# Latent attention walked chunk by chunk of queries: VectorE sums the weights in PSUM, GpSimd makes the low parts, the value products run three tiles behind the scores

## The chip, the cores and the metric

The kernel is one program on one core of a Trainium2 chip. Its time is the device time of one execution in microseconds, the median of several runs. The core has TensorE (PE: matmuls, and PEld: their weight loads), VectorE (DVE), ScalarE (ACT), GpSimd (POOL) and SyncE (SP, which here issues DMAs). Each engine works through its own list of instructions in order, and waits at an instruction whose inputs or whose buffer are not ready.

## The reference, cut to what matters

One encoder layer over 1024 rows of one request and 256 of another. The part in question is the latent attention (MLA), 16 heads:

```
s = (einsum('bqhd,bkhd->bhqk', qn_b, k_nope) + einsum('bqhr,bkr->bhqk', qr_b, k_rope)) * scale
p = softmax(s, axis=-1)
o = einsum('bhqk,bkhd->bqhd', p, v)          # 16 heads, V_DIM 64, QK 64 + 32
```

The other parts (projections, dilated attention, gates, convolutional feed-forward, norms) are the same instructions in the same order on every engine before and after.

## The kernel before, in words

Products are made in three passes of float32r: an operand is split into a high part (a rounded copy) and a low part (the exact value minus the high part), and high x high, high x low and low x high are summed in PSUM.

The latent attention keeps the scores with keys on the partitions and queries along the row. A tile of scores is 128 keys x 512 queries. A head has 8 key tiles x 2 chunks of 512 queries for the long request, and one tile that holds both key blocks of the short one: 17 tiles a head, 272 in all. A tile takes these steps:

- three matmuls into a bank of tag `S` (`Head.scores`, L1171 to L1173); the third one also adds minus the row's maximum, from row 96 of `qL`
- `soft` (L1123): ACT makes `p` = exp (L1125) and `ph`, the same exp rounded to float32r (L1126); then the low part `pl` = `p` - `ph` (`sub_dve`, a helper on L78)
- the sum of the weights over the key tiles: POOL copies the first `p` of a chunk to `acc` (L1195) and adds the others (`pool_tt`, helper on L81); in the last two heads DVE adds every fourth
- the value products: two matmuls, `ph` and `pl`, into the `O` bank of that chunk (L1214, L1215); the weights of the matmul are `V`, high and low part side by side, so rows 0 to 63 and 64 to 127 of `O` are added at the end (`finish_o`: ACT L1135, then DVE)

Before, key tiles are the outer loop and the two chunks the inner one, so both chunks' `O` banks are open through a head; `pend` puts the value products of one key tile (two tiles of scores) behind the scores of the next.

`fill` puts other work between the tiles: the row maxima of the next head (`row_max`: one matmul into a bank of tag `mi`, L1106, and a `reduce_max` by DVE, L1107; at the end the two short ones, L1111 and L1112, a small maximum `nm`, and a transpose on PE, L1115, which ACT copies to `mr`), the projections of a later pair of heads (`project_pair`, into `mi` banks, L1076, which ACT and DVE split into `kH`/`kL` or `qH`/`qL`), and the sums of `acc` over partitions (`row_sums`, L1146). PSUM has eight banks: 3 `S`, 3 `mi`, 2 `O`. A scheduler orders each engine's instructions ahead of the run; the order on each engine is fixed in the program.

`value_load` (L1044) brings `V` for a pair of heads, one DMA of 10 KB a partition, two buffers.

Of the kernel before, what the change touches and what calls it, by code (L numbers as in the profile page):

```python
# [46 lines left out]
def kernel(  # L47
# [111 lines left out]
    def ada_chunk(c, load, banks_, tile_):  # L159
        """columns [512c, 512c+512) of the modulation, as per-partition columns of modT"""  # L160
        *ps, tp = banks_()
        tp = tp.rearrange("p (b n) -> p b n", b=4)
        for k in range(KD):
            j = k % 4
            w = load()
            nc.sync.dma_start(out=w, in_=ada_w[k * P:(k + 1) * P, 512 * c:512 * c + 512])
            nc.tensor.matmul(ps[k // 4][32 * j:32 * j + 32, :], lhsT=cT[:, k, :], rhs=w, start=True, stop=True,
                             tile_position=(0, 32 * j))
        rows = tile_()
        nc.scalar.copy(out=rows, in_=ps[0])  # L170
# [44 lines left out]
    # Winograd's form of Strassen's product: halves of the contraction, of a pair of blocks of features, of the tokens  # L215
# [6 lines left out]
    class Halves:  # L222
        """one split operand after another"""
# [30 lines left out]
    def product_set(raw, dst, mid, early=False):  # L254
        """dst = the product for two blocks of features"""
# [29 lines left out]
    # modulation, first norm, transposed activations  # L285
# [23 lines left out]
    def banks():  # L309
        """PSUM of a modulation chunk"""  # L310
# [73 lines left out]
    def values0(w):  # L384
        """values of the first group"""
# [37 lines left out]
    # projections: queries and keys of the dilated attention, latents; the values of the other groups meanwhile  # L423
# [19 lines left out]
    def sums(j):  # L443
        """the operands' sums, of one tile of each half of the contraction"""
# [56 lines left out]
    # dilated attention, gates  # L501
# [36 lines left out]
    def value_rows(g, b):  # L538
        """rows of a block of values"""
# [17 lines left out]
    def queries_keys(pair, g, res):  # L557
        """in the order of the classes, split"""
# [13 lines left out]
    def window(g, i):  # L572
        """first key of the window, query offset in it, value blocks as (index, column, keys)"""
# [21 lines left out]
    def block(w, to, m=P):  # L595
        """a block of features, multiplied plainly"""
# [24 lines left out]
    def rope(x, c, co, si, tiles):  # L621
        """rotation and split, in two steps"""
# [13 lines left out]
    def norms():  # L636
        """latents' norms, rotated part of the keys"""
# [84 lines left out]
    def gather(pair, full, gs):  # L722
        """least scores and sums of the groups, in the order of the tokens"""
# [16 lines left out]
    def combine(pair, full):  # L740
        """joint softmax weights of the three groups, merged output"""
# [174 lines left out]
    # the second branch's output projection, values of the latent attention, rotated parts of its queries  # L916
# [21 lines left out]
    def values_out(q, bank, stage, w):  # L938
        """split values of four heads, to DRAM"""
# [19 lines left out]
    def rope_q(j, w):  # L959
        """rotated parts of four heads' queries, to DRAM"""  # L960
# [62 lines left out]
    # latent attention  # L1023
# [6 lines left out]
    RATE = (3600, 700, 960, 960)  # L1030

    def mi():
        return mk(psM[1], [P, 512], tag="mi", bufs=3)
# [10 lines left out]
    def value_load(p_):  # L1044
        vts[p_] = mk(mpl, [P, NT, 2, 2, 64], F32R, tag="V", bufs=2)
        nc.sync.dma_start(out=f32(vts[p_]), in_=f32(v_d)[p_])
# [76 lines left out]
    def soft(ps):  # L1123
        p_, ph, pl = ms(tag="p", bufs=3), ms(F32R, "ph", 3), ms(F32R, "pl", 3)
        nc.scalar.activation(out=p_, in_=ps, func=AF.Exp, scale=MSCALE)  # L1125
        nc.scalar.activation(out=ph, in_=ps, func=AF.Exp, scale=MSCALE)  # L1126
        sub_dve(pl, p_, ph)
# [32 lines left out]
    class Head:  # L1160
        def __init__(self, h):
            self.h, self.hh = h, h % 2
            self.q, self.k, self.v = qts[h], kts[h], vts[h // 2]
# [11 lines left out]
        def w(self, kt):  # L1175
            return self.v[:, kt, self.hh].rearrange("p s d -> p (s d)")

        def step(self, kt, fill):
            """scores and weights of one key tile, or of the short group at the end"""
            got = []  # L1180
            if kt == NS:
                ps = mk(psM[1], [P, 512], tag="S", bufs=3)
                for j in range(2):
                    self.scores(ps[:, 256 * j:256 * j + 256], NS + j, SS, 256)
                e = soft(ps)
                pool_tt(self.acc[:, SS:T], e[0][:, 0:256], e[0][:, 256:512], ALU.add)
                fill()
                return [e]
            for c in range(2):
                ps = mk(psM[1], [P, 512], tag="S", bufs=3)  # L1190
                self.scores(ps, kt, 512 * c, 512)
                e = soft(ps)
                a = self.acc[:, 512 * c:512 * c + 512]
                if kt == 0:
                    nc.gpsimd.tensor_scalar(out=a, in0=e[0], scalar1=1.0, scalar2=1.0, op0=ALU.mult, op1=ALU.mult)  # L1195
                else:
                    (dve_tt if self.h >= NH - 2 and (2 * kt + c) % 4 == 3 else pool_tt)(a, a, e[0], ALU.add)
                got.append(e)
                fill()
            return got  # L1200

        def values(self, kt, es):
            if kt == NS:
                op = mk(psM[1], [P, 512], tag="O", bufs=2)
                for j in range(2):
                    for q in range(2):
                        nc.tensor.matmul(op[:, 0:256], lhsT=self.w(NS + j), rhs=es[0][1 + q][:, 256 * j:256 * j + 256],
# [3 lines left out]
            if kt == 0:  # L1211
                self.o = [mk(psM[1], [P, 512], tag="O", bufs=2) for _ in range(2)]
            for c in range(2):
                nc.tensor.matmul(self.o[c], lhsT=self.w(kt), rhs=es[c][1], start=(kt == 0), stop=False)  # L1214
                nc.tensor.matmul(self.o[c], lhsT=self.w(kt), rhs=es[c][2], start=False, stop=(kt == NS - 1))  # L1215
                if kt == NS - 1:
                    finish_o(self.o[c], self.h, 512 * c, 512)
# [6 lines left out]
    def stage(i):  # L1224
        return ms(F32R, ("ph", "pl", "p")[i % 3], 3)

    def ahead(jobs):
        """each job's weights are loaded before the job in front of it runs"""
# [24 lines left out]
    def prep(k, cs, stage, dst):  # L1253
        """normalised, split output of pair k for some chunks"""
# [96 lines left out]
    pend = None  # L1351
    for h in range(NH):
# [16 lines left out]
    pend[0].values(pend[1], pend[2])  # L1369
# [19 lines left out]
    # gated merge  # L1389
# [59 lines left out]
    def pa_early(m):  # L1449
        """weights in tiles that the later chunks' outputs take"""  # L1450
# [53 lines left out]
    # output projection, second norm  # L1504
# [38 lines left out]
    # the tokens are halved into (first half of the long request, of the short one) and the rest: HT columns each  # L1543
# [6 lines left out]
    def second(c, x2s):  # L1550
        """transposes of a chunk's rows, modulated; first halves are split"""
# [51 lines left out]
    # convolutional feed-forward, up: Winograd's form of Strassen's product, with the halves of the contraction,  # L1603
    # of a pair of blocks of features, and of the tokens
# [14 lines left out]
    def up_load(col):  # L1619
        """both halves of the contraction of two blocks of features, one of each half of them"""  # L1620
# [21 lines left out]
    # the first two blocks are multiplied plainly, while the operands' sums are made  # L1642
# [44 lines left out]
    def acts(p_, tt):  # L1687
        """the operands of the down product"""
# [52 lines left out]
    # down, in the same form, with the halves of the features, of the columns, and of the tokens; final norm  # L1741
# [97 lines left out]
    def gated(x, i, j, hs, ssq=None, early=False):  # L1839
        """half of the columns of x2 + gate * x"""  # L1840
# [132 lines left out]
```

## Time and profile before

| | |
|---|---|
| median of 3 runs | 2578.05 us (2569.92 to 2586.26) |
| the profiled execution, span of the program | 2573.2 us |
| latent attention, first scores to last value products | 895.8 to about 1461 us: 565 us |
| PE busy in that stage | 507.4 us of 565.2 |
| DVE busy in that stage | 531.8 us |
| POOL, ACT busy in that stage | 396.9 us, 354.7 us |

The profiled execution is given by its span; it lies 4.9 us below the median, inside the range of the runs. A matmul's end is modelled: one of 512 columns shows as 0.39 to 0.40 us, while the next one starts 0.23 us after it. So PE can be idle although its row of busy time is full, and waits of PE below about 0.16 us don't show. The head starts of the stage (first scores of each head) are at 895.83, 934.41, 969.67, 1000.20, 1040.35, 1070.97, 1109.58, 1140.14, 1180.33, 1211.02, 1249.61, 1280.20, 1316.07, 1346.76, 1382.33 and 1421.01 us.

### The profile page before, as it was taken

What the parts mean: (1) busy time and instruction counts of PE and PEld (TensorE: products, weight loads), DVE (VectorE), ACT (ScalarE), POOL (GpSimd) and SP (SyncE); (2) the same over time, 40 slices, a digit from 0 to 9 for tenths busy, and PEclk for the clock granted to TensorE, in tenths of its full rate; (3) what the DMA queues carried; (4) which work ended last, traced back from release to release, by engine and by line L of the source; (5) the groups of instructions that cost most, each with busy time, mean ns of one, the idle gap of its engine ahead of it and who ended that gap; (6) DMA issues with size and microseconds to landing.
All of it is one profiled execution on the core that took longest, in us unless ns stands there. A gap on an engine that the chain in (4) does not pass through costs nothing. (4 is left out here: it accounts for less than half of the span.)

```text
span 2573.2 us, 37087 instructions
## 1 busy us (share of the span) xinstructions
PE 2425.6 (94%) x13177; PEld 2009.6 (78%) x13177; DVE 1620.4 (63%) x2477; ACT 1085.4 (42%) x2106; POOL 1176.5 (46%) x826
## 2 busy tenths in 40 slices
PE   7899999999999989999998889998999999999997
PEld 4799996655578766666665678787999999988876
DVE  5733333343447799999999852548556556567668
ACT  4422123444434456666665543344223223244434
POOL 1543331100125177676777553026555654638473
PEclk9999999999999999999999899998999999999998
DMA  7233226566367923233332474351322322357554
GB/s 253 58 117 103 91 90 212 156 192 217 104 178 249 314 53 78 75 78 80 80 77 65 104 223 140 129 162 43 106 86 86 105 78 80 102 206 244 180 179 159
DMA packets 255187, 342.88 MB, mean 133 GB/s; under 512 B 24269, under 2 KB 157150, under 8 KB 253978
## 3 DMA queue, kind: packets, MB, share of 16 engines
q1 hardware_dynamic: 229358, 311.40, 39.2%
q10 hardware_dynamic: 25644, 29.12, 3.3%
q8 instruction: 103, 1.69, 0.3%
q14 instruction: 82, 0.67, 0.1%
HBM read 237.06 MB, written 94.19 MB: 129 GB/s over the span
## 5 line engine op out<-in xcount | busy, mean ns | idle before, releaser
L244 PE MATMUL X<-t,wh 128*128 128x320 f32 x2864 | 539.6, 310 | 8.0 <-ACT wh L230 4.1
L244 PEld LDWEIGHTS X<-t,wh 128*128 128x128 f32 x2864 | 452.2, 189 | 8.9 <-ACT wh L230 4.4
L81 POOL TENSOR_TENSOR acc<-acc,p 128x512 f32<-128x512 f32 x216 | 326.6, 1529 | 93.3 <-ACT p L1125 89.1
L244 PE MATMUL X<-t,wl 128*128 128x320 f32 x1432 | 328.2, 310 | 6.3 <-DVE wl L78 6.3
L78 DVE TENSOR_TENSOR pl<-p,ph 128x512 fp32r<-128x512 f32 x272 | 307.5, 1144 | 10.8 <-ACT ph L1126 8.8
L244 PEld LDWEIGHTS X<-t,wl 128*128 128x128 f32 x1432 | 240.2, 189 | 7.3 <-DVE wl L78 6.7
L1125 ACT ACTIVATE p<-S 128x512 f32<-128x512 f32 x272 | 163.6, 601 | 121.6 <-PE S L1173 63.5
L81 POOL TENSOR_TENSOR wl<-wr,wh 128x512 fp32r<-128x512 f32 (+2 forms) x50 | 68.1, 1363 | 301.8 <-ACT wh L209 272.0
L100 PE MATMUL pp<-t,wh 128*128 128x512 f32 (+3 forms) x672 | 199.8, 378 | 3.1 <-DVE sm L892 2.6
L78 DVE TENSOR_TENSOR ut<-X,ut 128x640 f32<-128x640 f32 x126 | 101.5, 820 | 138.3 <-PE X L244 85.8
L230 ACT CAST wh<-wr 128x512 fp32r<-128x512 f32 x113 | 70.1, 621 | 272.9 <-PE X L244 183.4
L1107 DVE TENSOR_REDUCE m<-mi 128x1 f32<-128x512 f32 x256 | 171.5, 681 | 17.7 <-PE mi L1106 16.7
L1126 ACT ACTIVATE ph<-S 128x512 fp32r<-128x512 f32 x272 | 162.9, 599 | 20.5 <-PE O L1214 20.2
L81 POOL TENSOR_TENSOR wl<-R,wh 128x512 fp32r<-128x512 f32 x63 | 103.3, 1640 | 145.4 <-ACT wh L230 145.4
L1798 PE MATMUL Y<-bh,ah 128*128 128x512 f32 x385 | 152.0, 395 | 7.7 <-DVE ut L78 6.6
L1798 PE MATMUL Y<-bl,ah 128*128 128x512 f32 x385 | 152.1, 395 | 6.3 <-POOL bl L81 6.3
L100 PEld LDWEIGHTS pp<-t,wh 128*128 128x128 f32 (+1 forms) x672 | 111.3, 185 | 56.4 <-issue 28.4
L1798 PE MATMUL Y<-bh,al 128*128 128x512 f32 x385 | 151.6, 394 | 0.0
L78 DVE TENSOR_TENSOR wl<-wr,wh 128x512 fp32r<-128x512 f32 x119 | 112.2, 943 | 53.5 <-ACT wh L230 48.9
L244 PE MATMUL X<-R,wh 128*128 128x320 f32 x736 | 139.3, 311 | 0.0
L78 DVE TENSOR_TENSOR pt<-X,pt 128x640 f32<-128x640 f32 x60 | 48.6, 823 | 135.2 <-PE X L244 83.8
L78 DVE TENSOR_TENSOR al<-ar,ah 128x640 fp32r<-128x640 f32 x75 | 89.2, 1191 | 59.7 <-ACT ah L1772 57.1
(438 smaller groups left out, 5773.3 us busy)
## 6 DMA issues: line engine op xcount, KB each, us to landing
ac_d<-ut SPq DMA_DIRECT2D x77, 320.0 KB
ar<-ac_d SPq DMA_DIRECT2D x75, 320.0 KB
R<-in_w_up_dram SPq DMA_DIRECT2D x84, 256.0 KB
br<-in_w_down_dram SPq DMA_DIRECT2D x77, 256.0 KB
ad<-in_ada_w_dram SPq DMA_DIRECT2D x64, 256.0 KB
wr<-in_w_in_dram SPq DMA_DIRECT2D x48, 256.0 KB
rw<-in_w_in_dram SPq DMA_DIRECT2D x20, 512.0 KB
V<-v_d SPq DMA_DIRECT2D x8, 1280.0 KB
```

Source lines behind the costliest of these rows:

```text
L78: nc.vector.tensor_tensor(out=out, in0=a, in1=b, op=op)
L81: nc.gpsimd.tensor_tensor(out=out, in0=a, in1=b, op=op)
L100: nc.tensor.matmul(ps, lhsT=w[k], rhs=x[k], start=(k == 0 and w is wh and x is xh), stop=(k == n - 1 and w is wl))
L230: nc.scalar.copy(out=h, in_=a)
L244: nc.tensor.matmul(ps[:, z, 0:320], lhsT=a[:, k, :], rhs=b[q][k][:, 320 * z:320 * z + 320], start=(j == 0 and i == 0), stop=(j == n - 1 an ...
L1107: nc.vector.reduce_max(out=m2[:, i, c:c + 1], in_=ps, axis=AX.X)
L1125: nc.scalar.activation(out=p_, in_=ps, func=AF.Exp, scale=MSCALE)
L1126: nc.scalar.activation(out=ph, in_=ps, func=AF.Exp, scale=MSCALE)
L1798: nc.tensor.matmul(ps, lhsT=a[:, P * j:P * j + P], rhs=b, start=(f == 0 and a is ah and b is bh), stop=(f == HF - 1 and a is al))
```

## The change

The chunk of queries becomes the outer loop: eight key tiles of chunk 0, eight of chunk 1, then the tile of the short request. One `O` bank is open at a time. The value products of a tile are issued after the scores of the third tile behind it (`LAG` 3).

The low parts `pl` of key tiles 1 to 7 go to POOL (224 of 272); those of key tile 0 and of the short tile stay on DVE. The sum of the weights goes to DVE: key tile 0 is only remembered, key tile 1 is added to it into a PSUM bank of the new tag `ac`, key tiles 2 to 6 are added in that bank in place, key tile 7 is added from the bank into `acc` in SBUF. That is 14 adds a head, 224 in all, of which 32 have both inputs in SBUF and 192 have the running sum in PSUM. POOL's 32 copies and 216 adds, and DVE's 8, go; the 16 adds of the short tile stay on POOL.

The bank for `ac` comes from `mi`, which has 2 banks now. `p`, `ph`, `pl` have 4, 5, 5 buffers (3 each before). `V` is loaded head by head, 16 DMAs of 640 KB in runs of 512 bytes, after the fifth tile of the head before.

```
+    PB, LAG = (4, 5, 5), 3
     def mi():
-        return mk(psM[1], [P, 512], tag="mi", bufs=3)
+        return mk(psM[1], [P, 512], tag="mi", bufs=2)
...
-    def value_load(p_):
-        vts[p_] = mk(mpl, [P, NT, 2, 2, 64], F32R, tag="V", bufs=2)
-        nc.sync.dma_start(out=f32(vts[p_]), in_=f32(v_d)[p_])
+    def value_load(h):
+        vts[h] = mk(mpl, [P, NT, 2, 64], F32R, tag="V", bufs=2)
+        nc.sync.dma_start(out=f32(vts[h]), in_=f32(v_d)[h // 2][:, :, h % 2])
...
-    def soft(ps):
-        p_, ph, pl = ms(tag="p", bufs=3), ms(F32R, "ph", 3), ms(F32R, "pl", 3)
+    def soft(ps, sub):
+        p_, ph, pl = ms(tag="p", bufs=PB[0]), ms(F32R, "ph", PB[1]), ms(F32R, "pl", PB[2])
         nc.scalar.activation(out=p_, in_=ps, func=AF.Exp, scale=MSCALE)
         nc.scalar.activation(out=ph, in_=ps, func=AF.Exp, scale=MSCALE)
-        sub_dve(pl, p_, ph)
+        sub(pl, p_, ph)
...
+        def step(self, c, kt):
+            ps = mk(psM[1], [P, 512], tag="S", bufs=3)
+            if c == 2:
                 for j in range(2):
                     self.scores(ps[:, 256 * j:256 * j + 256], NS + j, SS, 256)
-                e = soft(ps)
+                e = soft(ps, sub_dve)
                 pool_tt(self.acc[:, SS:T], e[0][:, 0:256], e[0][:, 256:512], ALU.add)
...
+            self.scores(ps, kt, 512 * c, 512)
+            e = soft(ps, sub_pool if kt else sub_dve)
+            if kt == 0:
+                self.first = e[0]
+            elif kt == 1:
+                self.sum = mk(psM[1], [P, 512], tag="ac", bufs=1)
+                dve_tt(self.sum, self.first, e[0], ALU.add)
+            else:
+                dve_tt(self.sum if kt < NS - 1 else self.acc[:, 512 * c:512 * c + 512], self.sum, e[0], ALU.add)
+            return e
...
+            nc.tensor.matmul(self.o, lhsT=self.w(kt), rhs=e[1], start=(kt == 0), stop=False)
+            nc.tensor.matmul(self.o, lhsT=self.w(kt), rhs=e[2], start=False, stop=(kt == NS - 1))
+            if kt == NS - 1:
+                finish_o(self.o, self.h, 512 * c, 512)
...
-    pend = None
+    pend = []
...
-        if h % 2 == 0 and h // 2 + 1 < KD:
-            value_load(h // 2 + 1)
         hd = Head(h)
-        for kt in range(NS + 1):
-            es = hd.step(kt, fill)
-            if pend is not None:
-                pend[0].values(pend[1], pend[2])
-            pend = (hd, kt, es)
+        for c, kt in [(c, kt) for c in range(2) for kt in range(NS)] + [(2, 0)]:
+            pend.append((hd, c, kt, hd.step(c, kt)))
+            fill()
+            if (c, kt) == (0, LAG + 1) and h + 1 < NH:
+                value_load(h + 1)
+            if len(pend) > LAG:
+                p_ = pend.pop(0)
+                p_[0].values(*p_[1:])
```

The lines of the helpers move by two or three: L1106 is L1107 after the change, L1214 is L1210, L1173 is L1174.

How the order moves, first on PE, in the middle of head 2 (heads are counted from 0). The row maximum and a projection stand between the scores `S` and the value products `O`; `waits` names the engine whose semaphore an instruction waits for. Before, two tiles' value products stand together, one behind the other chunk's:

```order
L1171 MATMUL S_1975_9560<-qH_1733_8757,kH_1716_8692 128x512 [waits Activation_49]
L1172 MATMUL S_1975_9560<-qH_1733_8757,kL_1717_8693 128x512
L1173 MATMUL S_1975_9560<-qL_1734_8758,kH_1716_8692 128x512
L1106 MATMUL mi_1979_9571<-kH_1731_8749,qH_1755_8843 128x512 [waits DVE_49]
L1076 MATMUL mi_1974_9556<-t_1413_7343,wh_1829_9079 128x256
L1076 MATMUL mi_1974_9556<-t_1416_7346,wh_1829_9079 128x256
L1076 MATMUL mi_1974_9556<-t_1413_7343,wl_1830_9080 128x256
L1214 MATMUL O_1957_9499<-ph_1961_9510,V_1703_8663 128x512
L1215 MATMUL O_1957_9499<-pl_1962_9511,V_1703_8663 128x512
L1214 MATMUL O_1958_9500<-ph_1966_9529,V_1703_8663 128x512 [waits Activation_49]
L1215 MATMUL O_1958_9500<-pl_1967_9530,V_1703_8663 128x512 [waits DVE_49]
```

Now, at the same place:

```order
L1172 MATMUL S_1980_9561<-qH_1733_8755,kH_1715_8689 128x512 [waits Activation_49]
L1173 MATMUL S_1980_9561<-qH_1733_8755,kL_1716_8690 128x512
L1174 MATMUL S_1980_9561<-qL_1734_8756,kH_1715_8689 128x512
L1107 MATMUL mi_1984_9572<-kH_1731_8747,qH_1755_8842 128x512 [waits DVE_49]
L1077 MATMUL mi_1979_9555<-t_1413_7343,wh_1830_9070 128x256
L1077 MATMUL mi_1979_9555<-t_1416_7346,wh_1830_9070 128x256
L1077 MATMUL mi_1979_9555<-t_1413_7343,wl_1831_9071 128x256
L1210 MATMUL O_1962_9499<-ph_1965_9507,V_1861_9166 128x512
L1211 MATMUL O_1962_9499<-pl_1966_9508,V_1861_9166 128x512 [waits Pool_49]
L1172 MATMUL S_1985_9580<-qH_1733_8755,kH_1715_8689 128x512 [waits Activation_49]
L1173 MATMUL S_1985_9580<-qH_1733_8755,kL_1716_8690 128x512
```

Every tile's scores are now followed by one tile's value products, those of three tiles earlier (`pl_1966` belongs to `S_1963`, the third `S` tile in front of `S_1980`), and the second of them waits for POOL where it waited for DVE. While the projection's `mi_1979` is open, one `mi` bank is left for the row maxima.

On DVE, in head 5, before: low parts `pl` (both inputs in SBUF) alternate with the reductions of the row maxima.

```order
L1107 TENSOR_REDUCE m2_2231_10419<-mi_2290_10600 128x1 [waits PE_49]
L78 TENSOR_TENSOR pl_2284_10576<-p_2282_10574,ph_2283_10575 128x512 [waits Activation_49]
L78 TENSOR_TENSOR pl_2289_10595<-p_2287_10593,ph_2288_10594 128x512 [waits PE_49,Activation_49]
L1107 TENSOR_REDUCE m2_2231_10419<-mi_2297_10620 128x1
L78 TENSOR_TENSOR pl_2296_10615<-p_2294_10613,ph_2295_10614 128x512 [waits DVE_49,PE_49,Activation_49]
L78 TENSOR_TENSOR pl_2302_10633<-p_2300_10631,ph_2301_10632 128x512 [waits PE_49,Activation_49]
L1107 TENSOR_REDUCE m2_2231_10419<-mi_2303_10638 128x1
```

Now the add of a tile's weights into `ac`, which waits for ACT's `p` of that tile, stands in front of the reduction of the row maximum that PE makes right behind the same tile's scores:

```order
L78 TENSOR_TENSOR ac_2289_10554<-ac_2289_10554,p_2300_10597 128x512 [waits DVE_49,Activation_49]
L1108 TENSOR_REDUCE m2_2244_10425<-mi_2303_10604 128x1 [waits PE_49]
L78 TENSOR_TENSOR ac_2289_10554<-ac_2289_10554,p_2306_10614 128x512 [waits DVE_49,Activation_49]
L1108 TENSOR_REDUCE m2_2244_10425<-mi_2309_10621 128x1 [waits PE_49]
L78 TENSOR_TENSOR ac_2289_10554<-ac_2289_10554,p_2313_10636 128x512 [waits DVE_49,Activation_49]
L1108 TENSOR_REDUCE m2_2244_10425<-mi_2316_10643 128x1 [waits PE_49]
```

Over the whole stage, 256 row maxima of 512 columns take an `mi` bank. After the change 93 of them take the bank that the row maximum just before used, and 107 that of the second before; with three banks one of them does the first, 75 the second and 121 the bank of the third before.

## Rows read from the trace of the kernel before

**Rows 1.** The page's first part: span, then busy time of each engine.

```profile
span 2573.2 us, 37087 instructions
PE 2425.6 (94%) x13177; PEld 2009.6 (78%) x13177; DVE 1620.4 (63%) x2477; ACT 1085.4 (42%) x2106; POOL 1176.5 (46%) x826
```

**Rows 2.** Busy time by stretch: stage, heads 4, 7, 14; columns named by its first line.

```profile
core 0: us, PE busy (x) PEld busy (x) DVE busy (x) ACT busy (x) POOL busy (x), PEclk, DMA share, GB/s
895.83:1461.00 565.17, 507.35 (x2158) 369.47 (x2156) 531.81 (x672) 354.70 (x692) 396.93 (x287) 0.96 0.29 74
...
1040.35:1070.97 30.62, 29.62 (x140) 21.94 (x138) 29.87 (x40) 21.43 (x43) 23.06 (x18) 1.00 0.55 139
...
1140.14:1180.33 40.19, 35.09 (x138) 25.71 (x137) 35.95 (x47) 22.41 (x45) 25.54 (x20) 0.92 0.07 19
...
1382.33:1421.01 38.68, 31.95 (x115) 19.92 (x113) 37.13 (x45) 22.60 (x44) 25.20 (x18) 0.87 0.24 73
```

**Rows 3.** Waits of PE and PEld in the stage: total us, times, longest.

```profile
PE O L1215 <- DVE pl L78: 15.5, 23, 1.9
PE mi L1115 <- DVE nm L1112: 14.2, 7, 3.0
PE mi L1106 <- DVE m L1107: 10.4, 14, 1.8
PE mi L1076 <- DVE kL L78: 3.1, 6, 0.6
PE O L1214 <- DVE ms L78: 2.3, 6, 0.4
...
PEld O L1215 <- DVE pl L78: 39.9, 60, 2.3
```

**Rows 4.** Groups by line and form, stage: count, busy us, mean ns, idle before.

```profile
L81 POOL TENSOR_TENSOR acc<-acc,p 128x512 f32<-128x512 f32 x216 | 326.6, 1529 | 93.3 <-ACT p L1125 89.1 <-PE mi L1076 1.9 <-DVE acc L78 1.3
L78 DVE TENSOR_TENSOR pl<-p,ph 128x512 fp32r<-128x512 f32 x272 | 307.5, 1144 | 10.8 <-ACT ph L1126 8.8
...
L1107 DVE TENSOR_REDUCE m<-mi 128x1 f32<-128x512 f32 x234 | 157.0, 681 | 17.6 <-PE mi L1106 16.7
...
L1195 POOL TENSOR_SCALAR acc<-p 128x512 f32<-128x512 f32 x32 | 23.3, 728 | 53.7 <-ACT p L1125 53.7
...
L78 DVE TENSOR_TENSOR acc<-acc,p 128x512 f32<-128x512 f32 x8 | 9.8, 1223 | 0.0
L78 DVE TENSOR_TENSOR nm<-m 128x8 f32<-128x8 f32 x15 | 9.6, 639 | 0.2
L78 DVE TENSOR_TENSOR kL<-mi,kH 128x512 fp32r<-128x512 f32 x14 | 9.6, 684 | 0.2
```

**Rows 5.** Timeline, head 7: start us, us, engine, line, names, count, idle before.

```profile
1156.44 0.50 PE L1106 MATMUL mi<-kH,qH 96*128 96x512 f32 x1 [1.17 <-DVE m L1107]
...
1156.91 1.80 DVE L78 TENSOR_TENSOR pl<-p,ph 128x512 fp32r<-128x512 f32 x1
...
1157.93 0.40 PE L1172 MATMUL S<-qH,kL 96*128 96x512 f32 x1
...
1158.17 0.40 PE L1173 MATMUL S<-qL,kH 97*128 97x512 f32 x1
...
1158.65 0.60 ACT L1125 ACTIVATE p<-S 128x512 f32<-128x512 f32 x1 [0.78 <-PE S L1173]
...
1159.24 0.67 DVE L78 TENSOR_TENSOR pl<-p,ph 128x512 fp32r<-128x512 f32 x1
...
1161.52 1.34 POOL L81 TENSOR_TENSOR acc<-acc,p 128x512 f32<-128x512 f32 x1 [0.47 <-PE mi L1076]
1161.63 0.68 DVE L1107 TENSOR_REDUCE m<-mi 128x1 f32<-128x512 f32 x1
```

**Rows 6.** Timeline, end of head 7's row maxima.

```profile
1164.27 1.83 DVE L78 TENSOR_TENSOR pl<-p,ph 128x512 fp32r<-128x512 f32 x1
...
1166.02 1.22 DVE L78 TENSOR_TENSOR nm<-m 128x8 f32<-128x8 f32 x1
...
1167.96 0.38 PE L1115 MATMUL mi<-t,nm 128*10 128x128 f32 x1 [2.11 <-DVE nm L1112]
```

**Rows 7.** Busy time in the stretch right behind, columns as in Rows 2.

```profile
1167.96:1174.79 6.83, 6.83 (x17) 5.36 (x18) 4.08 (x5) 2.55 (x5) 2.55 (x2) 0.51 0.01 2
```

More of the change, by code (lines that the diff above doesn't have):

```diff
@@ L1162, in __init__ @@
             self.h, self.hh = h, h % 2
-            self.q, self.k, self.v = qts[h], kts[h], vts[h // 2]
+            self.q, self.k, self.v = qts[h], kts[h], vts[h]
             self.acc = accs[h] = mk(mpl, [P, T], tag="acc", bufs=3)
@@ L1175, in w, with values @@
         def w(self, kt):
[L1176 to L1182, printed above, removed]
+            return self.v[:, kt].rearrange("p s d -> p (s d)")
+        def step(self, c, kt):
+            ps = mk(psM[1], [P, 512], tag="S", bufs=3)
+            if c == 2:
                 for j in range(2):
                     self.scores(ps[:, 256 * j:256 * j + 256], NS + j, SS, 256)
-                e = soft(ps)
+                e = soft(ps, sub_dve)
                 pool_tt(self.acc[:, SS:T], e[0][:, 0:256], e[0][:, 256:512], ALU.add)
[L1187 to L1203, printed above, removed]
+                return e
[8 more added lines that the diff above has]
+                dve_tt(self.sum if kt < NS - 1 else self.acc[:, 512 * c:512 * c + 512], self.sum, e[0], ALU.add)
+            return e
+        def values(self, c, kt, e):
+            if c == 2:
                 op = mk(psM[1], [P, 512], tag="O", bufs=2)
@@ L1206, in values @@
                     for q in range(2):
-                        nc.tensor.matmul(op[:, 0:256], lhsT=self.w(NS + j), rhs=es[0][1 + q][:, 256 * j:256 * j + 256],
+                        nc.tensor.matmul(op[:, 0:256], lhsT=self.w(NS + j), rhs=e[1 + q][:, 256 * j:256 * j + 256],
                                          start=(j == 0 and q == 0), stop=(j == 1 and q == 1))
@@ L1211, in values @@
             if kt == 0:
[L1212 to L1217, printed above, removed]
+                self.o = mk(psM[1], [P, 512], tag="O", bufs=2)
+            nc.tensor.matmul(self.o, lhsT=self.w(kt), rhs=e[1], start=(kt == 0), stop=False)
+            nc.tensor.matmul(self.o, lhsT=self.w(kt), rhs=e[2], start=False, stop=(kt == NS - 1))
+            if kt == NS - 1:
+                finish_o(self.o, self.h, 512 * c, 512)
     ready = set()
@@ L1224, in stage @@
     def stage(i):
-        return ms(F32R, ("ph", "pl", "p")[i % 3], 3)
+        return ms(F32R, ("ph", "pl", "p")[i % 3], PB[(1, 2, 0)[i % 3]])
     def ahead(jobs):
@@ L1358 @@
         side = [others(h), 0.0, 0.0, (h > 0) + max(0, h - NH + 3)]
-        if h % 2 == 0 and h // 2 + 1 < KD:
-            value_load(h // 2 + 1)
         hd = Head(h)
-        for kt in range(NS + 1):
-            es = hd.step(kt, fill)
-            if pend is not None:
-                pend[0].values(pend[1], pend[2])
-            pend = (hd, kt, es)
+        for c, kt in [(c, kt) for c in range(2) for kt in range(NS)] + [(2, 0)]:
[6 more added lines that the diff above has]
+                p_[0].values(*p_[1:])
         if h % 2 == 0 or h == NH - 1:
             run(side[0])
-    pend[0].values(pend[1], pend[2])
+    for p_ in pend:
+        p_[0].values(*p_[1:])
     zc = mk(mpl, [P, 2 * NT], tag="zc", bufs=2)
```

## The prediction, made before the changed kernel ran

> **What bounds the kernel now.** The page's first part [rows 1] shows PE busy for 94% of the span, which would make any saving on DVE worthless. But that is a mean over stages. The next view to read is busy time by stretch [rows 2]: in the latent attention DVE is busy 531.8 of 565.2 us, 94%, and PE 507.4. Head 7 takes 40.2 us, head 4 only 30.6: in both DVE is nearly full, and in head 7 PE is busy 35.1 of 40.2 at a mean granted clock of 0.92.
>
> How far PE is from its own limit needs the timeline, since busy rows of PE overlap: a matmul of 512 columns follows the one before after 0.23 us (second and third pass of a score tile) [rows 5]. By the program the stage has 768 of them for scores (3 for each of 256 tiles), 512 for values, 234 for row maxima [rows 4] and 210 for projections (7 pairs of heads, 15 matmuls for each of 2 chunks): 1724 x 0.23 = 397 us. Those of 256 columns are 96 + 64 + 30 + 105 = 295, at half of that 34 us; row sums and transposes I put at 25: about 455 us. So 110 of the 565 us are not work of PE. The granted clock explains a part: a mean of 0.96 [rows 2] is 4% lost, 23 us. The rest is waiting, and the list of waits [rows 3] says for whom: every large row of PE ends in DVE. DVE sets the pace of this stage, and PE is next.
>
> Why DVE is full is seen in two groups [rows 4]: 272 low parts at 1144 ns and 234 reductions at 681. Both have 512 elements a partition. The timeline shows the difference [rows 5]: a low part takes 0.67 us in one place and 1.80 in another, while a reduction that reads PSUM takes 0.68 with a POOL add running beside it. The low part reads two SBUF tiles; where POOL works on SBUF too, one waits for the other. POOL shows the other side: its add is 1.34 us beside the reduction [rows 5], 1529 ns in the mean [rows 4]. Head 7's end shows it at its worst [rows 6]: a low part of 1.83, then a maximum over 8 elements that takes 1.22, and PE stands 2.11 us at the transpose behind them; right after, the clock is granted at 0.51 for 6.8 us [rows 7].
>
> **The change, part by part.** The sum is made for the profiled execution, 2573.2 us, in this stage alone; outside it no order changes.
>
> *DVE's work.* 224 low parts go, 224 x 1.144 = 256, and 8 adds, 10. Of the 224 new adds, 32 read two SBUF tiles: 1.144 each, 37. The other 192 read the sum in PSUM. No row of before writes PSUM from DVE. The nearest is `kL<-mi,kH`, one input in PSUM and one in SBUF, at 684 ns; the dear end is the 1223 ns of the in-place add `acc<-acc,p` on DVE [rows 4]. I take 0.684, because the costly part is the second SBUF read and that is what goes: 131. DVE falls from 532 to 532 - 266 + 168 = 434 (537 at the dear end, the same as now).
> The Trainium skill (Perfetto Trace Analysis, Optimizing Scalar/DVE Operations) gives DVE a fixed overhead of some 60 ns an instruction on SBUF and 125 on PSUM. That is 65 ns more for each of the 192, 12 us as an estimate, and if all of it came onto the path the sum below would be -29 instead of -41; the rows here, 0.684 with PSUM against 0.67 for a low part alone, show no such difference.
>
> *POOL's work.* It loses 326.6 + 23.3 us [rows 4] and gets 224 low parts, two SBUF inputs each like its adds: 1.34 beside reductions, 1.53 in the mean of before. DVE's partners that read two SBUF tiles fall from 17 or more a head to 5 and the small maximum, so I take 1.34: 300. POOL goes from 397 to 347 (389 at the dear end): not the bound. ACT keeps its 355. The longest is then PE with 455.
>
> *What PE gets back.*
> 1. Waits of the value products for `pl` [rows 3]: 15.5 us by PE's rows. As a matmul's row is 0.16 us longer than its pitch, each of the 23 hides 0.16, 4 more; the weight loads show 37 further waits of which at most 0.16 each, 6, can be lost. 25 in all, between 15.5 and the 39.9 of the loads. All of it goes: from the third score pass to `p` are 0.48 us, two exponentials 1.2 [rows 5], the low part 1.34 to 1.8; ready after 3.0 to 3.5 us, wanted after three tiles, over 5. **-25**.
> 2. The transpose of the maxima: 14.2 us in 7 waits. Of head 7's 2.11 the low part's excess in front of `nm` goes, but `nm` reads two SBUF tiles and still meets POOL. **-9**, between 0 and -14.
> 3. The clock: the half clock stands behind these waits [rows 6, 7]. With half of the wait, about half of the 23: **-12**, between 0 and -23.
> 4. Late `kL`, `ms` and smaller ones, 5.4 in the rows shown, 3 more hidden under the pitch: **-5**, between 0 and -8.
> 5. Two `mi` banks instead of three. PE waits 10.4 us for `mi` now, 14 times. After the change 93 maxima follow the last one's reduction in the same bank. That reduction stands on DVE behind the tile's add, which waits for `p`: 1.08 us after the third score pass `p` is done, +0.68 add, +0.68 reduction, 2.45. PE's next maximum comes 6 matmuls (1.4 us) later without a projection between, 9 (2.1 us) with one. So up to 1.05 is short, but one wait delays the next tile's scores too and so pays for the next; and where PE's order puts the maximum behind the value products, nothing is short. 0.1 us each: **+9**; between 0 and, at the 1.17 us of the row [rows 5], +109.
> 6. At the end of the stage three tiles' value products stand behind the last scores instead of two: **+1**. `V` is issued 12 tiles, some 20 us, ahead of its use and moves half as much a time, in shorter runs; SP issues it when the value products of the head before last are done, which they are by then, so nothing queues behind it: 0.
>
> Sum: -25 - 9 - 12 - 5 + 9 + 1 = **-41**: a span of 2532. The span of before stands 4.9 us below the median of the runs, so **2537 us**. The stage would take 524 us, PE's 455 with 13% lost.
>
> **Rivals.**
> *The two `mi` banks bind (slower).* Without term 5 the change gives back 50. With 93 tight maxima it is lost when each costs 0.54 us more; at the 1.17 of the row [rows 5] it is 109 - 50 = +59, 2637 us. For it: the chain through the add is longer than a tile's matmuls, projections hold the other bank through most heads. Against: the waits overlap, and before, with 98% of DVE used in head 4, PE still was busy 29.6 of 30.6. I give 0.11 to slower, 0.12 to a cost near break-even (0.3 to 0.8 us each: 2556 to 2602).
> The Trainium skill (Perfetto Trace Analysis, Matmuls) wants independent groups of matmuls to rotate through different PSUM banks, so that evacuating one overlaps the next; taking a bank from `mi` goes against it, and the 1.17 us wait agrees.
>
> *DVE and POOL only swap.* If the add into PSUM meets POOL as the low part did, the 192 cost 1.144, DVE keeps 522 of its 532 us, and only 10 us come back: 2568. For it: no row shows DVE writing PSUM. Against: reading PSUM keeps 0.68 beside POOL. 0.10.
> The Trainium skill (the same page, Optimizing Scalar/DVE Operations) says that moving work between these two might not help, since they share an SBUF read port; the 1.80 and 0.67 us agree that they do, but its rule does not look at where the operands lie.
>
> *PE becomes the bound and runs through.* All of `pl` by the loads' rows 40, `nm` 14, clock 23, late ones 8, `mi` no dearer: -85, 2493. The stage would be at 480, PE at 95%. Head 4 of before comes near: 29.6 of 30.6 busy. 0.12 for under 2513.
>
> **The numbers.** My forecast, 2513 to 2552, has 0.55. A measurement here tells about 1% from no change, 26 us: faster is below 2552, slower above 2604. Faster: 0.55 + 0.12 = 0.67. Same: 0.12 + 0.10 = 0.22. Slower 0.11. The range reaches from 2500, which leaves out 0.06 of the best case, to 2590, which leaves out the slower rival: 0.12.
>
> **What would show it.** Adds named `ac` at 0.68 us on DVE, not 1.1; low parts on POOL at 1.3 to 1.4; no wait of the value products for POOL worth naming; DVE busy about 434 in the stage, 83% of it; odd heads down from 39 to some 34 us, even ones unchanged or a little longer; the transpose's wait near 1 us and fewer stretches at half clock. The forecast is wrong if the row maxima's wait for DVE exceeds 30 us in PE's rows, if `ac` adds cost over 1 us, or if POOL is busy over nine tenths and the value products wait for it.

## The result and the profile after

The changed kernel takes 2507.3 us (median of 4 runs, 2504.9 to 2509.3), the kernel before in the same comparison 2574.4 (4 runs, 2569.9 to 2586.3). The ratio is 0.9732, 95% interval 0.9711 to 0.9753: 67 us less, where 41 were forecast and 2500 to 2590 us was the range. It lies below the 2513 to 2552 us that the prediction calls its forecast, in the part under 2513 that it gave 0.12. A second comparison gave 2507.8 us, ratio 0.9738 (0.9716 to 0.9760).

The page's first part answers to [rows 1]:

```profile
span 2505.9 us, 37001 instructions
PE 2396.6 (96%) x13177; PEld 2006.3 (80%) x13177; DVE 1508.6 (60%) x2469; ACT 1081.3 (43%) x2106; POOL 1114.5 (44%) x802
```

Its PE row says as little as that of before: 94% became 96% with the same 13177 matmuls. The stage shows the change. Busy time by stretch, columns as in [rows 2]: the stage, then heads 4, 7 and 14.

```profile
906.60:1393.40 486.80, 470.57 (x2148) 361.07 (x2146) 416.37 (x661) 349.97 (x692) 335.04 (x263) 0.99 0.34 89
1027.96:1057.35 29.39, 29.34 (x140) 22.27 (x139) 24.70 (x41) 21.49 (x44) 18.55 (x15) 1.00 0.52 127
1117.80:1148.26 30.46, 30.09 (x137) 23.75 (x136) 27.22 (x45) 21.81 (x44) 21.50 (x17) 1.00 0.14 40
1321.80:1357.40 35.60, 28.89 (x119) 19.57 (x118) 32.36 (x46) 23.62 (x49) 27.84 (x22) 0.95 0.36 107
```

The stage fell from 565.2 to 486.8 us, 78 less, and DVE in it from 531.8 to 416.4. Head 7 is down from 40.2 to 30.5 us, head 4 from 30.6 to 29.4; its PE is now busy 29.34 of 29.39. Head 14 is now the dearest. The clock of the stage went from 0.96 to 0.99. That the time fell by 67 and not 78 lies ahead of the stage: it begins at 906.6 us instead of 895.8, at a mean granted clock up to there of 0.97 instead of 0.98. In the eleven traces of the experiments below it begins between 900.3 and 906.6, at 903.6 in the one of the kernel before with one number changed. So I take this for scatter and not for a doing of the change. The 78 of the stage, from one trace of each kernel, is uncertain by a few us: a second trace of the changed kernel has 490.5 us. Behind the last value products the span is the same to 0.5 us: 1113.5 and 1113.1 (the two stretches end 1.3 and 0.6 us behind them).

Waits of PE and PEld in the stage, to be laid beside [rows 3] (total us, times, longest):

```profile
PE O L1211 <- POOL pl L81: 4.0, 6, 1.0
PE mi L1116 <- DVE nm L78: 3.3, 7, 0.8
PE O L1210 <- issue: 2.5, 1, 2.5
...
PE mi L1112 <- DVE m L1108: 1.3, 1, 1.3
PE mi L1077 <- DVE m L1108: 1.0, 2, 0.8
...
PEld mi L1107 <- DVE m L1108: 12.4, 42, 0.8
PEld O L1211 <- POOL pl L81: 9.5, 14, 1.5
```

The value products waited 15.5 us for a low part, now 4.0 (loads: 39.9, now 9.5). The transposes waited 14.2, now 3.3. The row maxima waited 10.4 us for a bank, with three banks; with two, no row of PE for them is left among the large ones.

Groups by line and form, to be laid beside [rows 4] (count, busy us, mean ns, idle before):

```profile
L81 POOL TENSOR_TENSOR pl<-p,ph 128x512 fp32r<-128x512 f32 x224 | 298.0, 1339 | 135.8 <-ACT ph L1127 110.3 <-PE mi L1107 4.8 <-PE S L1173 4.6
...
L1108 DVE TENSOR_REDUCE m<-mi 128x1 f32<-128x512 f32 x234 | 159.3, 686 | 32.4 <-PE mi L1107 29.8
L78 DVE TENSOR_TENSOR ac<-ac,p 128x512 f32<-128x512 f32 x160 | 111.0, 694 | 9.1 <-ACT p L1126 7.1
L78 DVE TENSOR_TENSOR pl<-p,ph 128x512 fp32r<-128x512 f32 x48 | 40.1, 836 | 9.3 <-ACT ph L1127 6.9 <-ACT qH L1083 0.7 <-POOL pl L81 0.6
L78 DVE TENSOR_TENSOR ac<-p,p 128x512 f32<-128x512 f32 x32 | 24.9, 780 | 0.8 <-ACT p L1126 0.8
L78 DVE TENSOR_TENSOR acc<-ac,p 128x512 f32<-128x512 f32 x32 | 22.0, 686 | 2.6 <-ACT p L1126 1.6
```

The three kinds of add point to the mechanism: with the running sum in PSUM 686 to 694 ns, with both inputs in SBUF 780. And POOL idles 136 us in front of its low parts, most of it until ACT has made the next `ph`: it is early, not late.

The end of head 7's row maxima, where [rows 6] had 1.83, 1.22 and 2.11 us, on DVE and then on PE (start us, us):

```profile
1140.28 0.73 DVE L78 TENSOR_TENSOR nm<-m 128x8 f32<-128x8 f32 x1
1140.93 0.69 DVE L78 TENSOR_TENSOR ac<-ac,p 128x512 f32<-128x512 f32 x1
```

```profile
1141.06 0.28 PE L1116 MATMUL mi<-t,nm 128*10 128x128 f32 x1 [0.37 <-DVE nm L78]
```

The maximum over 8 elements still meets POOL (0.73 us; 0.17 in the mean where POOL is nearly idle, in the experiment with all low parts on DVE), but nothing long stands in front of it. The transpose waits 0.37 us instead of 2.11, and the half clock that followed [rows 7] is gone.

### The profile page after: what moved, and what is told of

Read it like the earlier page. It is cut to its first block, busy times and chain, and to the rows that moved or that the text cites. A ratio compares the mean times of both kernels' runs of the same rounds, so it can differ in the third digit from the quotient of the medians.

```text
span 2505.9 us, 37001 instructions
## 1 busy us (share of the span) xinstructions
PE 2396.6 (96%) x13177; PEld 2006.3 (80%) x13177; DVE 1508.6 (60%) x2469; ACT 1081.3 (43%) x2106; POOL 1114.5 (44%) x802
## 5 line engine op out<-in xcount | busy, mean ns | idle before, releaser
L81 POOL TENSOR_TENSOR pl<-p,ph 128x512 fp32r<-128x512 f32 x224 | 298.0, 1339 | 135.8 <-ACT ph L1127 110.3
L81 POOL TENSOR_TENSOR wl<-wr,wh 128x512 fp32r<-128x512 f32 (+2 forms) x50 | 62.9, 1258 | 310.7 <-ACT wh L209 281.2
L100 PE MATMUL pp<-t,wl 128*128 128x512 f32 (+3 forms) x336 | 123.2, 367 | 0.0
```

The costliest lines, as they stand in the source:

```text
L81: nc.gpsimd.tensor_tensor(out=out, in0=a, in1=b, op=op)
L100: nc.tensor.matmul(ps, lhsT=w[k], rhs=x[k], start=(k == 0 and w is wh and x is xh), stop=(k == n - 1 and w is wl))
```

## The experiments

The theory (A): before, DVE is full, because its low parts read two SBUF tiles beside a POOL that does the same; the sum in PSUM and the low parts on POOL take it out of the limit, and three tiles of distance cover POOL's slower low part. The rivals: the order and the distance alone do it (B); it does not matter where the sum lies (C); and, from the prediction, the two `mi` banks cost. Ratios are to the kernel before; its median was 2575.5 us.

**The value products one tile behind.**

```
-    PB, LAG = (4, 5, 5), 3
+    PB, LAG = (4, 5, 5), 1
```

> The changed kernel with the value products one tile behind the scores (LAG 1) in place of three. Theory A (VectorE's pace was set by instructions that read two SBUF tiles beside GpSimd; the sum in PSUM frees it, TensorE becomes the bound): a low part is ready some 3.1 us after the third score pass (0.48 to p, 1.2 for two exponentials, 1.34 on GpSimd); with one tile of lag two tiles then take at least 3.1 + 0.23 + 0.7 = 4.0 us, 2.0 a tile for the 1.79 of now, so +40 to +65 us on 2507: 2545 to 2575. Theory B (the lag is what gave the gain, the swap of work is even): all of the gain goes, 2575 or more, and the waits of the value products for the low parts account for all of it.

Measured: 2568.7 us, ratio 0.9979 (0.9970 to 0.9988). The stage's busy times (columns as in [rows 2], here and in all such rows below):

```profile
902.99:1454.88 551.89, 505.91 (x2148) 355.41 (x2146) 415.89 (x661) 353.83 (x691) 335.29 (x263) 0.99 0.31 78
```

Its waits for the low part:

```profile
PE O L1211 <- POOL pl L81: 37.3, 72, 1.3
...
PEld O L1211 <- POOL pl L81: 93.5, 151, 1.7
```

The time is in A's range. DVE is as free as in the changed kernel (415.9 us), and all but 7 us of the gain are lost: the new split of the engines is worth little without the distance. A low part on POOL takes 1.33 us instead of DVE's 0.7, and PE's loads now wait for it 151 times. (The load of `V` hangs on `LAG` too; it moves from behind the fifth tile to behind the third.)

**The new order with the old engines.** Low parts on DVE, sum on POOL in SBUF, three `mi` banks; chunk order, distance of three and buffers of the change.

```
-            e = soft(ps, sub_pool if kt else sub_dve)
+            e = soft(ps, sub_dve)
+            a = self.acc[:, 512 * c:512 * c + 512]
...
-                dve_tt(self.sum if kt < NS - 1 else ..., self.sum, e[0], ALU.add)
+                (dve_tt if self.h >= NH - 2 and (8 * c + kt) % 4 == 3 else pool_tt)(a, a, e[0], ALU.add)
```

> The changed order (chunk by chunk, lag 3, V by head, the buffers of the change) with the work of VectorE and GpSimd as before: all low parts on VectorE, the sum on GpSimd in SBUF, three mi banks (the ac bank isn't needed). Theory A: VectorE is busy about 530 us in the stage again and the stage is near 540 to 560 us; only the waits for low parts (about 25 us) can go: 2545 to 2572. Theory B: the order and the lag carry the gain: 2505 to 2525.

Measured: 2557.6 us, ratio 0.9942 (0.9921 to 0.9962), in A's range. The stage, and PE's largest wait:

```profile
902.05:1442.37 540.32, 493.55 (x2143) 370.93 (x2141) 503.45 (x667) 350.84 (x691) 395.69 (x287) 0.95 0.31 80
```

```profile
PE O L1209 <- DVE pl L78: 14.8, 15, 5.5
```

Theory B falls: order and distance alone bring 18 us of the 67. DVE is busy 503.5 of 540.3 us, the low part takes 1046 ns in the mean, and PE still waits 14.8 us for it.

**The running sum in SBUF**, the same adds on the same engine:

```
-                self.sum = mk(psM[1], [P, 512], tag="ac", bufs=1)
+                self.sum = self.acc[:, 512 * c:512 * c + 512]
```

> The changed kernel with one thing undone: VectorE keeps the running sum in SBUF (acc) and not in PSUM, so all 224 adds read two SBUF tiles. Same counts on every engine, mi still 2 banks. Theory A: adds take 1.1 to 1.3 us for 0.69, low parts on GpSimd 1.5 to 1.65 for 1.34, VectorE is busy about 510 us: 2540 to 2570. Rival C (the gain is that the work is spread evenly; where the sum lies does not matter): 2505 to 2515, adds at 0.7.

Measured: 2564.7 us, ratio 0.9963 (0.9950 to 0.9975). C falls. In the stage (547.8 us) DVE is busy 499.1. The two groups that meet:

```profile
L81 POOL TENSOR_TENSOR pl<-p,ph 128x512 fp32r<-128x512 f32 x224 | 336.3, 1513 | 151.5 <-ACT ph L1127 125.4 <-PE O L1211 11.4 <-PE S L1173 8.8
L78 DVE TENSOR_TENSOR acc<-acc,p 128x512 f32<-128x512 f32 x192 | 219.2, 1142 | 7.1 <-ACT p L1126 4.5
```

And the largest waits, of PE and of its loads:

```profile
PE mi L1107 <- DVE m L1108: 20.1, 43, 1.7
...
PEld mi L1107 <- DVE m L1108: 55.8, 94, 2.2
```

The same add costs 1142 ns instead of 690, the low part on POOL 1513 instead of 1339, and DVE is full again. Putting this one tile back costs 57 us. Taking away the distance cost 61 and the engines' split 50: each part needs the others, so these figures do not divide the 67 among them. The Trainium skill (SBUF — State Buffer, Who interferes with whom) says that a DVE instruction with at most one SBUF input, outside the modes that use two ports, does not contend with GpSimd; the 694 ns beside these 1142 agree with it.

**Two `mi` banks in the kernel before.**

```
-        return mk(psM[1], [P, 512], tag="mi", bufs=3)
+        return mk(psM[1], [P, 512], tag="mi", bufs=2)
```

> The kernel before with two mi banks in place of three and nothing else. My prediction put +9 us on this in the changed kernel. If the cost of a bank depends on how late VectorE is, it is larger here, where VectorE is 94% busy: 2585 to 2615 (before 2574), with TensorE's waits for the row maxima well over 10 us. If two banks do whatever VectorE does, 2570 to 2580.

Measured: 2579.6 us, ratio 1.0015 (1.0003 to 1.0028). The stage, and the waits for `mi`:

```profile
903.65:1467.20 563.55, 512.33 (x2156) 354.91 (x2155) 527.82 (x670) 352.88 (x692) 392.42 (x287) 0.98 0.29 75
```

```profile
PE mi L1106 <- DVE m L1107: 14.5, 42, 1.2
...
PE mi L1115 <- DVE nm L78: 2.6, 3, 1.3
...
PE mi L1115 <- DVE nm L1112: 0.9, 4, 0.2
...
PEld mi L1106 <- DVE m L1107: 53.8, 105, 1.6
```

Two rows of the kernel before, beside those of [rows 3]:

```profile
PE mi L1115 <- DVE nm L78: 1.6, 3, 0.9
...
PEld mi L1106 <- DVE m L1107: 19.8, 24, 2.1
```

The waits of the row maxima grow (from 10.4 in PE's rows, from 19.8 in the loads'), but the stage stays at 563.5 us, and the time is in the range put for "two banks do whatever VectorE does". What PE loses at the maxima it gains at the transposes, which wait 3.5 us instead of 15.8: with DVE full, what PE waits for in one place it need not wait for in another. The expectation of a loss that grows with DVE's lateness was too high.

**All low parts on DVE**, the sum in PSUM:

```
-            e = soft(ps, sub_pool if kt else sub_dve)
+            e = soft(ps, sub_dve)
```

> The changed kernel with all 272 low parts of the stage on VectorE; the sum stays in PSUM, so GpSimd keeps only 16 small adds of the stage and the preparation of the next one. Theory A (low parts are long because GpSimd works on SBUF beside them; VectorE, when full, sets the pace): low parts fall to 0.67 to 0.72 us, and VectorE has 272 x 0.68 = 185, sums 155, reductions 159 and 59 of other work of the changed kernel, 558 us, more than the 532 of before: it is full again, stage 560 to 590, 2575 to 2605 us. Rival B2 (it is enough that the two engines no longer meet on SBUF; the move of the low parts is worth nothing in itself): the stage stays within 10 us of the changed kernel's 486, 2505 to 2520. Rival C2 (a low part is long for a reason of its own): it stays above 1.0 us, VectorE at 640 or more, 2650 and above.

Measured: 2587.1 us, ratio 1.0038 (1.0018 to 1.0058).

```profile
905.75:1468.45 562.70, 521.30 (x2148) 378.13 (x2146) 523.98 (x884) 349.32 (x691) 40.43 (x39) 0.93 0.29 77
```

The groups of the low parts and of the small maxima:

```profile
L78 DVE TENSOR_TENSOR pl<-p,ph 128x512 fp32r<-128x512 f32 x272 | 189.2, 696 | 8.0 <-ACT ph L1127 7.5
...
L78 DVE TENSOR_TENSOR nm<-m 128x8 f32<-128x8 f32 x15 | 2.5, 167 | 0.0
```

With POOL busy 40 us instead of 397 the same 272 low parts take 696 ns instead of 1144 [rows 4]: POOL was the reason. But with the sums on DVE too it is at 524 of 563 us, full again, without contention. B2 and C2 fall, and the time lies in A's range; the 558 us of DVE were put too high.

**Without the running sum.** It leaves out the adds; one tile plus 1 is written in the sum's place.

```
-            elif kt == 1:
-                self.sum = mk(psM[1], [P, 512], tag="ac", bufs=1)
-                dve_tt(self.sum, self.first, e[0], ALU.add)
-            else:
-                dve_tt(...)
+            elif kt == 1:
+                nc.vector.tensor_scalar(out=self.acc[:, 512 * c:512 * c + 512], in0=e[0], scalar1=1.0, scalar2=1.0, op0=ALU.mult, op1=ALU.add)
```

> The changed kernel without the running sum (left out: the adds of the weights; one tile of each chunk plus 1 is written in place of the sum, 32 instructions). VectorE loses about 155 us of its 416 in the stage. It asks what holds the changed kernel's stage at 486 us. Theory A (VectorE has left the limit, what remains is TensorE's own work and scattered waits): only part of the waits for row maxima and their transpose goes, 5 to 15 us, 2492 to 2503. Rival D (VectorE still sets the pace with 86% busy): heads fall towards TensorE's own 27.5 us, stage 450 to 460, 2470 to 2482.

**And the freed bank for `mi`**, `bufs=3` again, otherwise as the one without the sum:

> As the kernel without the sum, and the PSUM bank that the sum leaves free goes to the row maxima and projections, three banks instead of two. Theory A: the two banks cost nothing that can be measured, within 4 us of the kernel without the sum. Rival (the two banks of the change bind, as the prediction's term of +9 has it): 8 to 15 us faster than that kernel.

Measured: 2501.1 us, ratio 0.9698 (0.9670 to 0.9727), and with the third bank 2499.8, 0.9691 (0.9656 to 0.9725). The stages:

```profile
902.62:1382.21 479.59, 467.96 (x2148) 360.10 (x2146) 295.51 (x468) 349.45 (x691) 329.44 (x263) 1.00 0.34 90
```

```profile
900.35:1376.32 475.97, 463.64 (x2143) 365.02 (x2141) 298.20 (x467) 347.62 (x691) 330.47 (x263) 0.99 0.35 91
```

Taking another 121 us off DVE brings 6 us (the intervals of this kernel and the changed one overlap). Rival D falls: in the changed kernel DVE no longer sets the pace, and the third bank brings nothing that can be told from zero. Both kernels lack the add that the chain of term 5 goes through, so they do not price the bank in the changed kernel itself.

**All low parts on POOL.**

```
-            e = soft(ps, sub_pool if kt else sub_dve)
+            e = soft(ps, sub_pool)
...
-                e = soft(ps, sub_dve)
+                e = soft(ps, sub_pool)
```

> The changed kernel with the remaining 48 low parts (first tile of each chunk and the last tile of a head) on GpSimd too. GpSimd gets 48 x 1.3 = 62 us more, 412 of 486, VectorE loses 40 and has 376. Theory A (neither engine is full): within 6 us of the changed kernel, 2500 to 2513; waits of the value products for GpSimd grow from 5 to 8 or 10 us, the waits for row maxima shrink by as much. Rival E (GpSimd is the next limit): 2520 to 2540, the value products wait for GpSimd by 25 us or more in TensorE's rows.

Measured: 2517.3 us, ratio 0.9759 (0.9730 to 0.9788): between the two ranges, and the interval overlaps that of the changed kernel.

```profile
PE O L1211 <- POOL pl L81: 7.7, 12, 1.3
...
PEld O L1211 <- POOL pl L81: 15.2, 22, 1.7
```

The waits for POOL are close to what A expected (8 or 10 us in PE's rows), those for the row maxima did not shrink (13.7 us of the loads, 12.4 in the changed kernel), and the time is 4 us above its range. The stage is 493.6 us. DVE has room for the low parts of key tile 0, where it has no add, and POOL takes 1.33 us for each; whether the loss is real is not settled.

**Two tiles behind.**

```
-    PB, LAG = (4, 5, 5), 3
+    PB, LAG = (4, 5, 5), 2
```

> The changed kernel with the value products two tiles behind the scores instead of three (one tile measured 2569). A tile lasts about 1.7 us in the mean of the stage. By the rows of the changed kernel a low part is ready 0.5 + 1.2 + 1.34 = 3.0 us after the third score pass, more where GpSimd still has the one before: two tiles, 3.4 us, are just enough, three are 5.1. Theory A (what the lag must cover is this chain, and nothing else): some waits of the value products for GpSimd, 10 to 25 us by the weight loads, 2508 to 2522. Rival (the third tile is what the change lives on, because every wait also disturbs the order behind it): 2530 to 2550, with over 30 us of waits.

Measured: 2530.3 us (three of the four runs 2530 to 2531, one 2519.5), ratio 0.9817 (0.9792 to 0.9842), at the rival's lower end:

```profile
906.62:1411.53 504.91, 477.21 (x2148) 361.48 (x2146) 421.36 (x660) 351.48 (x691) 333.20 (x263) 0.99 0.33 86
```

The waits of the loads, those for POOL in the range that A expected:

```profile
PEld O L1211 <- POOL pl L81: 24.5, 34, 1.7
PEld mi L1107 <- DVE m L1108: 18.7, 35, 1.7
PEld mi L1112 <- DVE nm L1113: 7.0, 6, 1.2
```

Waits for POOL by the loads are 15 us more than with three tiles; beside them those for the row maxima grew by 6, and a wait of L1112 of 7 us is new. This fits a third tile that saves both the wait and what the wait does to the order behind it, 23 us together; the rival's 30 us of waits for POOL did not come. The kernel before was three tiles behind for chunk 0 and two for chunk 1, so this run does not divide the gain exactly: with the new engines two tiles give 45 us and the third 23, and with the old engines order, buffers and third tile together brought 18 (second experiment).

**The last head, and the changed kernel beside it.** Its low parts of key tiles 2, 4 and 6 go to DVE:

```
-            e = soft(ps, sub_pool if kt else sub_dve)
+            e = soft(ps, sub_pool if kt and not (self.h == NH - 1 and kt % 2 == 0) else sub_dve)
```

> The changed kernel once more, as the measure for the version beside it: 2505 to 2510.

> The changed kernel, in the last head with 6 of its 14 GpSimd low parts on VectorE (tiles 2, 4 and 6 of a chunk): there no row maxima are left for VectorE, GpSimd makes low parts for the next stage beside, and TensorE waits 3.0 us for it in three places, with 3.4 us at half clock behind. Theory A: these go, 1 to 5 us faster than the changed kernel in the same call. Rival: the low parts on VectorE meet those on GpSimd, become 1.4 to 1.8 us, and the wait changes its engine: no difference, or up to 3 us slower.

Measured side by side, 5 runs each: the changed kernel 2507.8 us, ratio to the kernel before 0.9738 (0.9716 to 0.9760); this version 2500.9, 0.9712 (0.9692 to 0.9733). From the five times of each, the difference of the means is 7.1 us, 95% interval 2.1 to 12.1: about 0.3% faster, more than the 1 to 5 expected. POOL's rows of the last head, of the changed kernel first:

```profile
1372.21 5.87 POOL L81 TENSOR_TENSOR pl<-p,ph 128x512 fp32r<-128x512 f32 x4
1378.59 1.28 POOL L81 TENSOR_TENSOR pl<-p,ph 128x512 fp32r<-128x512 f32 x1 [0.51 <-ACT ph L1127]
1380.31 6.26 POOL L81 TENSOR_TENSOR pl<-p,ph 128x512 fp32r<-128x512 f32 x5 [0.43 <-ACT ph L1127]
```

```profile
1373.18 1.49 POOL L81 TENSOR_TENSOR pl<-p,ph 128x512 fp32r<-128x512 f32 x1 [0.81 <-ACT ph L1127]
1376.00 1.29 POOL L81 TENSOR_TENSOR pl<-p,ph 128x512 fp32r<-128x512 f32 x1 [1.33 <-ACT ph L1127]
1377.96 1.40 POOL L81 TENSOR_TENSOR pl<-p,ph 128x512 fp32r<-128x512 f32 x1 [0.67 <-PE O L1210]
1380.14 1.29 POOL L81 TENSOR_TENSOR pl<-p,ph 128x512 fp32r<-128x512 f32 x1 [0.78 <-ACT ph L1127]
```

Without row maxima and projections a tile of the last head is so short that POOL, at 1.3 us a low part, runs without a gap and is the bound there. With six of them on DVE it has gaps, and the last head, from its first scores to its last value products, takes 31.9 us (1356.12 to 1387.99) against 35.4 and 38.4 in the two traces of the changed kernel. Of the kernels that compute the whole, this is the fastest.

## Why the prediction was right, and where its sum failed

The mechanism was right: DVE full, contention of two-SBUF reads, the sum in PSUM as the way out. The size was not, 67 instead of 41 us; that 2507 is inside the stated range is due to its lower end, put 13 us below the forecast's own band. The step that failed is **term 5** of the sum; terms 2, 3 and 4 were too small as well, and term 1 too large by 7.

PE's own work first. In the trace of after, 1712 matmuls of 512 columns at a distance of 0.232 us from start to start (the usual one there), 295 of 256 columns at 0.119, and 16 us from start to start for row sums, transposes and the 40 small ones at the end make 448 us; the forecast had 455. So the stage lost 117 us before and 39 now; the forecast left 69. For the terms I add up, in both traces, what each distance between two starts has above this, at full clock, by the producer that ended the wait:

| term | forecast | before, us | after, us | measured |
|---|---|---|---|---|
| 1: value products for `pl` | -25 | 24 | 6 | -18 |
| 2: transposes for `nm` | -9 | 18 | 5 | -13 |
| 3: clock | -12 | 18 | 3 | -15 |
| 4: late `kL`, `qL`, and `O` banks | -5 | 13 | 4 | -9 |
| 5: `mi` for the reductions | +9 | 18 | 5 | -13 |
| the rest, mostly below 0.2 us each | 0 | 19 | 12 | -7 |

The rows add up to -75 of the stage's -78; row sums and other small ones are not among them.

*Term 1.* As forecast in kind; the low part on POOL took 1339 ns, 1.34 was used. Not all of it went. Two tiles would not have done (23 us); the estimate of 3.0 to 3.5 us left no margin against two tiles of some 1.7.

*Terms 2 and 3.* The transpose waits 0.5 us each instead of the 1 expected. Half of the waits was assumed to keep half of the lost clock; with the waits nearly gone, the granted clock is at half for 3.4, 3.4 and 6.8 us of the whole stage. Each time a stall is near: 2.5 us at 1332, three waits for POOL of about 1 us from 1365 to 1374, the end of the head loop at 1391.

*Term 5.* It was priced from the chain add, reduction, maximum on a DVE that still has other work queued, and with a wait that the trace of before showed (1.17 us), on a DVE that was full. Its sign was wrong. How long PE waits there goes with how late DVE is, though not in strict order: waits of PE's loads for the reductions with two banks are 53.8 us with DVE at 528 us (the kernel before), 28.6 at 524 (all low parts on DVE), 55.8 at 499 (the sum in SBUF), 12.4 at 416 (the changed kernel), 7.6 at 296 (no sum). In time the bank cost 4 us in the kernel before, and a third one brought 1.3 us without the sum, inside the noise; the changed kernel with three was not run, since its eight banks are all taken. Terms 2 and 5 were not two prices: in the kernel before, taking the bank moved the wait from the transposes to the maxima at the same stage time. DVE's lateness stood behind both, and pricing the places apart kept waits that had lost their cause. How much of term 2's -13 is due to DVE and how much to the bank stays open, since two banks alone took the transposes from 15.8 to 3.5 us.

The rival in which *PE runs through* forecast a stage of 480 and 2493 us; the measured stage of 487 lies nearer to it than to the forecast's 524. That *DVE and POOL only swap* is what the sum in SBUF does, 2565 where 2568 was put for it. The rival of the *two banks* did not occur. What would show it: `ac` at 0.69 (0.68 said), `pl` on POOL 1.34 (1.3 to 1.4), as said; DVE at 416 (434), lower because the low parts and first adds left on it took 836 and 780 ns where 1144 was put; odd heads fell to 30.5 to 30.7 (head 13 to 24.0), further than the 34 said, and even ones did not get longer. "No wait for POOL worth naming" holds but for the last head.

What the Trainium skill (Perfetto Trace Analysis, Optimizing Scalar/DVE Operations) has of a larger overhead for PSUM, 12 us by the prediction's estimate from it, is not seen in the durations: 694 ns with the sum in PSUM against 696 for a low part from SBUF with POOL idle. Its rule that moving work between DVE and GpSimd might not help all but held in the kernel with the sum in SBUF (0.9963) and not in the one with it in PSUM (0.9732).

One view over the traces, the stage against DVE's busy time in it: 564 us with 528 (two banks, before), 563 with 524, 548 with 499, 540 with 503, then 487 with 416, 494 with 389, 480 with 296, 476 with 298. From some 500 up the stage is DVE's time plus 7 to 10%; at 416 and below it stays within 20 us. The two kernels with a shorter distance stand apart, 552 and 505 with 416 and 421: there POOL's latency decides.

About half of what is left in the stage lies in the last two heads: by the same sum, head 14 loses some 12 us and head 15 some 10, the others at most 2.6 each. DVE in head 14, around PE's largest wait of the stage (2.5 us, ended at 1332.35):

```profile
1328.07 1.77 DVE L78 TENSOR_TENSOR or<-or,or 128x512 f32<-128x512 f32 x1
1329.77 1.75 DVE L78 TENSOR_TENSOR ac<-p,p 128x512 f32<-128x512 f32 x1
1331.56 0.69 DVE L78 TENSOR_TENSOR ms<-O,ms 64x512 f32<-64x512 f32 x1
```

The view puts that wait to no releaser; the last of these rows, which frees the `O` bank, ends 0.1 us before it does, behind two instructions that read two SBUF tiles each beside POOL. No run took this one away, so the reading stays open.

## What to carry to other kernels

When one engine is full, the waits for it share one cause: price the change by asking whether the engine leaves the limit, and if it does, let all waits for it fall, instead of summing them one by one. Look at where operands lie before moving work between DVE and POOL: the same add was 0.69 us with the sum in PSUM and 1.14 with it in SBUF, and with that went 57 of the 67 us. A slower producer needs more distance to its consumer, and the last iterations, where the loop gets shorter, need their own split.

## What the runs showed of the hardware

- DVE adds into a PSUM bank in place, one input there and one in SBUF, 128 x 512: 693 to 695 ns, whether POOL works (changed kernel) or is nearly idle (all low parts on DVE).
- The same low part, two SBUF inputs, on DVE: 696 ns with POOL idle, 836 beside POOL's low parts, 1144 beside POOL's adds. POOL's own goes from 1339 to 1513 ns when DVE adds from SBUF beside it. Both lose.
- A maximum over 8 elements a partition, two SBUF inputs, takes 0.17 us in the mean with POOL nearly idle (all low parts on DVE), 0.64 in the kernel before and 0.53 in the changed one, and 1.22 in [rows 6]: beside POOL, the size of an instruction says little about its price.
